# One unit of seven products per feed-forward block in place of two, placed in the middle of the block

## Chip, cores and metric

The kernel runs on one core of a Trainium2 chip. The metric is the device time of one launch in microseconds (us). The stated time of the kernel before is the median of three runs; everything that is read from a trace comes from one profiled execution.

## The reference

Two networks follow one another on 256 tokens of width 1024, all in float32. The first has four layers (a feed-forward block, an attention mixer, a feed-forward block), the second two layers (a mixer, a feed-forward block). The ten feed-forward blocks (FFNs) all compute

```python
def swiglu(x, w_in, w_out):
    gate, up = jnp.split(x @ w_in, 2, axis=-1)      # x: 256 x 1024, w_in: 1024 x 5632
    return (jax.nn.silu(gate) * up) @ w_out          # w_out: 2816 x 1024
```

with a norm before and a norm or a gate after. Eight are those of the first network (`ffn_1`), two those of the second (`ffn_2`). Only they are touched by the change.

## The kernel before, in words

**Numbers in two parts.** A float32 matrix is split into a rounded part `hi` (a cast on ScalarE, L171) and the rest `lo` (a subtraction on VectorE, L172): `hilo`. A product is three matmuls, hi by hi, hi by lo and lo by hi (`mm3`, L215 to L224). Weights come by DMA into a ring of 4 raw buffers of 1 MB (`raw`, issued by SyncE, L182) and are split into a ring of 7 pairs of `hi`/`lo` tiles of 128 x 1024 (`W_BUFS = 7`), from which TensorE reads.

**Chunks.** The hidden width 2816 is cut into 11 chunks of 256. For a chunk `c` and a token tile `t` (two tiles of 128 tokens), `f1(c, t)` makes gate and up with 24 matmuls of 512 columns, `hidden` applies the activation (`th` on ScalarE, two `hd` steps on VectorE) and transposes the result to `hT`, and `f2(c, t)`, called by `pop`, adds the chunk's part of the output with 12 matmuls. A chunk's input weights are 4 tile pairs, its output weights 2.

**Units of seven.** Two neighbouring chunks, 512 columns of gate and 512 of up, can be made together: the two token tiles, the two halves of the depth 1024 and gate/up form a product of 2 x 2 by 2 x 2 blocks, and the generator `seven(c)` makes it with seven block products of 12 matmuls each in place of eight. The left factors, seven sums and differences of the blocks of x in two parts (`S`), are made once per FFN by `halves_of_x` on VectorE and ScalarE. The right factors are made by the DMA itself: a 1 MB quarter of the weights is loaded (`load`, SyncE) and another is added onto it in place (`plus`, two accumulating DMAs of 512 KB issued by GpSimd, L452), for two running buffers `rs` called `y` and `z`; two factors are bare quarters, loaded into the raw ring. A unit thus moves 8 MB where two plain chunks move 4 MB, and splits 14 tile pairs where they split 8. Each `next` of the generator makes one product (its split, its 12 matmuls, and what VectorE and ScalarE add up, gate and multiply behind it).

**Order.** The FFN's order is written out by hand. Chunks 0 and 1 come first, then twice (`PLAN`) a string of steps: two plain chunks and one unit, chunks (2, 3) with the unit 4, 5 and chunks (6, 7) with the unit 8, 9. In the string, `f` is one `f1`, `o` one `pop`, `7` one product of the unit, `n` the first loads of the next unit. Steps n = 7 and n = 15 also take an `ada_step` (1 MB of another weight and four VectorE multiply-adds, L1183; 32 such steps in all, four per FFN from the second FFN to the ninth). `middle()`, called after the first string, loads the gain of the norm after; in the first FFN it also does the late set-up (small DMAs and transposes), in the two of the second network it starts `start_gate`, four more multiply-adds of 1 MB each, spaced by the planner. Chunk 10 and the last output steps end the FFN. Tasks such as `hidden` are resumed by a planner's clock, counted from the matmuls written out so far: `yield 4.0` means 4 us of that clock later. On the engines the instructions do not follow the text strictly: in the trace, matmuls of a product and of a chunk alternate.

Of the kernel before, what the change touches and what calls it, by code (L numbers as in the profile page):

```python
# [18 lines left out]
P = 128  # L19
D = 1024  # L20
S = 256
NT = S // P
# [19 lines left out]
GATE_STEP = 9.0  # L42


PLAN = (((2, 3), 4), ((6, 7), 8))


def _constants():
# [54 lines left out]
class _Net:  # L103
# [296 lines left out]
    def ffn(self, w_in, w_out, factors, finish, middle, scaled):  # L400


        nc = self.nc
        hT, wi, wo, acc = {}, {}, {}, {}

        def f1(c, t):
            self.prepared(t)
            if c not in wi:
                wi[c] = self.load_in(w_in, [(c * FC, FC), (DFF + c * FC, FC)])
            self.start(hidden(c, t, self.project(t, wi[c], 2 * FC)))  # L410

        def hidden(c, t, ps):
            th = self.t(self.fp, [P, FC], "th")
            nc.scalar.activation(th, ps[:, :FC], AF.Tanh, scale=factors(t)[0])
            hd = self.t(self.fp, [P, FC], "hd", bufs=3)
            nc.vector.scalar_tensor_tensor(hd, th, 1.0, ps[:, :FC], op0=ALU.add, op1=ALU.mult)
            nc.vector.scalar_tensor_tensor(hd, hd, factors(t)[1], ps[:, FC:], op0=ALU.mult, op1=ALU.mult)
            yield 4.0
            hT[c, t] = self.to_hT(hd)

        def f2(*cs, t):
            for c in cs:
                if c not in wo:
                    wo[c] = self.load_out(w_out, c)
                self.force(lambda: (c, t) in hT)
            if t not in acc:
                acc[t] = self.accs(t)
            steps = [(hT[c, t], wo[c]) for c in cs]
            if cs[-1] == NCH - 1:
                self.last_steps(acc[t], steps)  # L430
            else:
                self.out_step(acc[t], *steps[0], cs[0] == 0, False)

        def seven(c):

            def quarter(k, n):
                return self.cols(w_in, c * FC + n * DFF, 512, 4 * k, 4)  # L440

            def load(k, n, alone=False):
                if alone:
                    r = self.t(self.wp, [P, 2 * UW], "raw", bufs=RAW_BUFS).rearrange("p (a b) -> p a b", a=4)
                else:
                    r = self.t(self.mp, [P, 4, 512], "rs", bufs=2)
                nc.sync.dma_start(r, quarter(k, n))
                return r

            def plus(r, k, n):  # L450
                for q in range(2):
                    nc.gpsimd.dma_start(r[:, 2 * q : 2 * q + 2], quarter(k, n)[:, 2 * q : 2 * q + 2], accum_op=ALU.add)  # L452

            def split(r):
                ws = []
                for q in range(2):
                    hi = self.t(self.wp, [P, UW], "hi", F32R).rearrange("p (a b) -> p a b", a=2)
                    lo = self.t(self.wp, [P, UW], "lo", F32R).rearrange("p (a b) -> p a b", a=2)
                    self.hilo(r[:, 2 * q : 2 * q + 2], hi, lo)
                    ws += [(hi[:, j], lo[:, j]) for j in range(2)]  # L460
                return ws

            def block(i, ws):
                ps, S = self.ps("mm"), sums["S"]
                x = ([S[0][:, i, k] for k in range(4)], [S[1][:, i, k] for k in range(4)])
                for k in range(4):
                    self.mm3([(ps, slice(0, 512))], x, k, ws[k], k == 0, k == 3)
                return ps

            def add(dst, u, v):  # L470
                nc.vector.tensor_tensor(dst, u, v, op=ALU.add)

            def tile(ps=None):
                r = self.t(self.mp, [P, 512], "sc", bufs=3)
                if ps is not None:
                    nc.scalar.copy(r, ps)
                return r

            def gate(g):
                th = self.t(self.fp, [P, 512], "res", bufs=2)  # L480
                nc.scalar.activation(th, g, AF.Tanh, scale=0.5)
                nc.vector.scalar_tensor_tensor(g, th, 1.0, g, op0=ALU.add, op1=ALU.mult)

            def out(t, g, u):
                nc.vector.scalar_tensor_tensor(u, g, -1.0, u, op0=ALU.mult, op1=ALU.mult)
                yield 6.0
                for i in range(2):
                    hT[c + i, t] = self.to_hT(u[:, FC * i : FC * i + FC])

            y = load(0, 1)  # L490
            plus(y, 0, 0)
            z = load(1, 1)
            yield
            u0 = tile(block(6, split(z)))
            plus(z, 0, 1)
            yield
            u1 = tile(block(3, split(y)))
            plus(y, 1, 1)
            add(u0, u0, u1)
            yield  # L500
            s = tile(block(0, split(load(0, 0, True))))
            yield
            g0 = self.t(self.fp, [P, 512], "res", bufs=2)
            add(g0, block(1, split(load(1, 0, True))), s)
            gate(g0)
            yield
            add(s, block(4, split(y)), s)
            plus(y, 1, 0)
            add(u0, u0, s)
            self.start(out(0, g0, u0))  # L510
            yield
            add(s, block(5, split(z)), s)
            add(u1, s, u1)
            yield
            add(s, block(2, split(y)), s)
            gate(s)
            self.start(out(1, s, u1))
            yield

        queue, sums = [], {}  # L520

        def pop():
            c, t = queue.pop(0)
            f2(c, t=t)

        first = ((0, 0), (0, 1), (1, 0), (1, 1)) if self.stage == 0 else ((0, 0), (1, 0), (0, 1), (1, 1))
        gens = [seven(c) for _, c in PLAN]
        next(gens[0])
        for c, t in first:
            f1(c, t)  # L530
        queue.extend((c, t) for c in range(2) for t in range(NT))
        self.start(self.halves_of_x(sums, scaled))
        for plain, c in PLAN:


            gen, after = gens.pop(0), gens[:1]
            others = [(r, t) for r in plain for t in range(NT)]
            for n, what in enumerate("fo77fo7o7fo7o7foo7no"):
                if what == "f":
                    f1(*others[0])  # L540
                    queue.append(others.pop(0))
                elif what == "o":
                    pop()
                elif what == "n":
                    for g in after:
                        next(g)
                else:
                    self.force(lambda: "S" in sums)
                    next(gen, 0)
                if n in (7, 15) and self.stage > 0:  # L550
                    self.ada_step()
            queue.extend((c + i, t) for i in range(2) for t in range(NT))
            if middle:
                middle()
                middle = None
        for t in range(NT):
            f1(NCH - 1, t)
        for t in range(NT):
            f2(NCH - 3, t=t)
            f2(NCH - 2, NCH - 1, t=t)  # L560
            finish(t, acc[t])
        self.drain()

    def halves_of_x(self, res, scaled):


        nc = self.nc
# [10 lines left out]
        def put(i, v):  # L578
            self.hilo(v, S_[0][:, i], S_[1][:, i])

        f = self.t(self.wp, [P, 2 * UW], "raw", bufs=RAW_BUFS).rearrange("p (a b) -> p a b", a=4)
        x = {}
        for t in (0, 1):
            for k in (0, 1):
# [3 lines left out]
                if not scaled:  # L588
                    nc.vector.tensor_tensor(v, v, rb[:, t, None, :].to_broadcast([P, 4, P]), op=ALU.mult)
        tt, stt = nc.vector.tensor_tensor, nc.vector.scalar_tensor_tensor  # L590
        put(0, x[0, 0])
        put(1, x[0, 1])
        put(2, x[1, 1])
        tt(x[1, 1], x[1, 1], x[1, 0], op=ALU.subtract)
        put(3, x[1, 1])
        tt(x[1, 0], x[0, 0], x[1, 0], op=ALU.subtract)
        put(5, x[1, 0])
        stt(x[0, 0], x[1, 1], -1.0, x[0, 0], op0=ALU.mult, op1=ALU.subtract)
        put(4, x[0, 0])
        stt(x[0, 1], x[0, 0], -1.0, x[0, 1], op0=ALU.mult, op1=ALU.subtract)  # L600
        put(6, x[0, 1])
        res["S"] = S_
        return
        yield
# [1005 lines left out]
```

## Time and profile before

| | |
|---|---|
| median of 3 runs | 2960.28 us (2956.38 to 2962.5) |
| the profiled execution | 2965.05 us, span of its trace 2963.3 us |
| busy: TensorE, VectorE, ScalarE, GpSimd | 2842.5, 2183.1, 1686.3, 427.2 us |
| the ten FFNs together | 1953 us of the span |
| read from HBM | 629.82 MB |

Busy time is the time in which an engine executes something. A window's row gives, for a stretch of the span, the busy time of each engine with its number of instructions, the granted clock of TensorE (1.00 is 2.4 GHz; a stretch that ran partly at 1.2 GHz shows a mean between 0.5 and 1), the busy share of the DMA engines (it can read a little over 1) and the rate. TensorE's busy time includes matmuls that ran at the lower clock, so what a stretch lost on TensorE is its idle time plus the length of the stretch times (1 - granted clock).

### The profile page before, as it was taken

How to read it: one execution, taken by the hardware profiler on the slowest of the kernel's cores; microseconds unless marked ns; L12 is line 12 of the kernel's file. 1: busy time of each engine (PE TensorE's matmuls, PEld its weight loads, DVE VectorE, ACT ScalarE, POOL GpSimd, SP SyncE). 2: the span in 40 equal slices, each digit the busy share in tenths (PEclk: the TensorE clock that was granted, in tenths of full speed). 3: DMA queues.
4: the chain of work that ended last, by engine and by line, in shares of the span. 5: the costliest groups of instructions: out<-in, count | busy, mean ns of one | idle time of the engine just before them, and what ended most of it. 6: DMA issues, size and time to landing. Idle time of an engine off the chain costs nothing. (4 is left out here: it accounts for less than half of the span.)

```text
span 2963.3 us, 36815 instructions
## 1 busy us (share of the span) xinstructions
PE 2842.5 (96%) x13165; PEld 2280.9 (77%) x13165; DVE 2183.1 (74%) x3275; ACT 1686.3 (57%) x2873; POOL 427.2 (14%) x601
## 2 busy tenths in 40 slices
PE   7999999999999999999999999999999998999998
PEld 5787777778787777878778777777778777788777
DVE  7676787877568887756877877587775687765777
ACT  6556655655665565556655556665554464544554
POOL 1112210211111011120211111221101110100110
PEclk9999999999999999999999999999999999999999
DMA  9864588796458879651697895469674599664794
GB/s 262 239 198 155 169 258 237 207 296 206 149 164 256 242 209 291 210 188 44 186 290 227 243 275 173 133 183 291 215 242 169 171 274 267 209 222 164 202 288 142
DMA packets 358043, 633.27 MB, mean 214 GB/s; under 512 B 15170, under 2 KB 190132, under 8 KB 357860
## 3 DMA queue, kind: packets, MB, share of 16 engines
q1 hardware_dynamic: 312724, 541.99, 53.5%
q0 software_dynamic: 44768, 88.30, 16.7%
q8 instruction: 104, 1.70, 0.2%
q14 instruction: 79, 0.65, 0.1%
q10 hardware_dynamic: 368, 0.62, 0.1%
HBM read 629.82 MB, written 1.05 MB: 213 GB/s over the span
## 5 line engine op out<-in xcount | busy, mean ns | idle before, releaser
L172 DVE TENSOR_TENSOR lo<-raw,hi 128x1024 fp32r<-128x1024 f32 x834 | 1000.1, 1220 | 232.5 <-ACT hi L171 223.6
L171 ACT CAST hi<-raw 128x1024 fp32r<-128x1024 f32 x834 | 859.3, 1051 | 322.4 <-PE mm L224 149.0
L220 PE MATMUL mm<-hi,xh 128*128 128x512 f32 (+2 forms) x1856 | 746.1, 404 | 10.3 <-ACT hi L171 5.6
L222 PE MATMUL mm<-lo,xh 128*128 128x512 f32 (+2 forms) x1856 | 730.7, 394 | 3.4 <-DVE lo L172 3.4
L224 PE MATMUL mm<-hi,xl 128*128 128x512 f32 (+2 forms) x1856 | 729.2, 393 | 1.9 <-DVE xl L172 1.0
L220 PEld LDWEIGHTS mm<-hi,xh 128*128 128x128 f32 x1856 | 350.8, 189 | 88.2 <-ACT hi L171 10.1
L224 PEld LDWEIGHTS mm<-hi,xl 128*128 128x128 f32 x1856 | 350.6, 189 | 78.3 <-DVE xl L355 4.8
L222 PEld LDWEIGHTS mm<-lo,xh 128*128 128x128 f32 x1856 | 351.4, 189 | 76.4 <-DVE lo L172 12.3
L171 ACT CAST hi<-rs 128x1024 fp32r<-128x1024 f32 x200 | 209.6, 1048 | 200.4 <-PE mm L224 150.0
L172 DVE TENSOR_TENSOR lo<-rs,hi 128x1024 fp32r<-128x1024 f32 x200 | 243.1, 1220 | 97.4 <-ACT hi L171 97.2
L452 POOL DMA_DIRECT2D rs<-in_ffn_w_in_dram x128 | 155.8, 1274 | 1101.7 <-DVE lo L172 650.9
L220 PE MATMUL mm<-hi,Sh 128*128 128x512 f32 x560 | 231.5, 413 | 13.3 <-ACT Sh L171 10.7
L222 PE MATMUL mm<-lo,Sh 128*128 128x512 f32 x560 | 227.4, 406 | 8.7 <-DVE lo L172 8.7
L224 PE MATMUL mm<-hi,Sl 128*128 128x512 f32 x560 | 224.0, 400 | 0.0
L264 ACT CAST hT<-tp 128x256 fp32r<-128x256 f32 x268 | 94.6, 371 | 204.1 <-PE tp L252 204.0
L222 PE MATMUL aA<-lo,hT 128*128 128x512 f32 x584 | 195.7, 398 | 7.7 <-DVE lo L172 7.7
L220 PE MATMUL aA<-hi,hT 128*128 128x512 f32 x584 | 197.3, 400 | 0.9 <-DVE s L657 0.9
L224 PE MATMUL aA<-hi,hT 128*128 128x512 f32 x584 | 196.2, 400 | 0.0
L222 PE MATMUL aB<-lo,hT 128*128 128x512 f32 x568 | 191.1, 396 | 0.0
L224 PE MATMUL aB<-hi,hT 128*128 128x512 f32 x568 | 190.1, 393 | 0.8 <-DVE hT L268 0.8
L220 PE MATMUL aB<-hi,hT 128*128 128x512 f32 x568 | 190.5, 398 | 0.0
L265 DVE TENSOR_TENSOR hT<-tp,hT 128x256 fp32r<-128x256 f32 x268 | 109.9, 418 | 85.8 <-ACT hT L264 84.5
(280 smaller groups left out, 3671.5 us busy)
## 6 DMA issues: line engine op xcount, KB each, us to landing
raw<-in_ffn_w_in_dram SPq DMA_DIRECT2D x224, 512.0 KB, 6.4
raw<-in_ffn_w_out_dram SPq DMA_DIRECT2D x88, 1024.0 KB, 6.7
rs<-in_ffn_w_in_dram POOLq DMA_DIRECT2D x128, 512.0 KB, 8.2
raw<-in_w_ada_dram SPq DMA_DIRECT2D x48, 1024.0 KB, 7.1
raw<-in_w_in_dram SPq DMA_DIRECT2D x44, 1024.0 KB, 5.2
rs<-in_ffn_w_in_dram SPq DMA_DIRECT2D x32, 1024.0 KB, 6.4
raw<-in_ffn_w_in_dram SPq DMA_DIRECT2D x32, 1024.0 KB, 5.9
raw<-in_w_ffn_in_dram SPq DMA_DIRECT2D x56, 512.0 KB, 5.6
```

Source lines behind the costliest of these rows:

```text
L171: self.nc.scalar.copy(hi, raw)
L172: self.nc.vector.tensor_tensor(lo, raw, hi.bitcast(F32), op=ALU.subtract)
L220: mm(ps, xh[k], wh[:, c], start=first, stop=False)
L222: mm(ps, xh[k], wl[:, c], start=False, stop=False)
L224: mm(ps, xl[k], wh[:, c], start=False, stop=last)
L264: nc.scalar.copy(hi, v)
L265: nc.vector.tensor_tensor(lo, v, hi.bitcast(F32), op=ALU.subtract)
L452: nc.gpsimd.dma_start(r[:, 2 * q : 2 * q + 2], quarter(k, n)[:, 2 * q : 2 * q + 2], accum_op=ALU.add)
```

## The change

`PLAN` becomes `PAIR = 6`: one unit per FFN, chunks 6 and 7; chunks 2, 3, 4, 5, 8 and 9 are plain. Chunks 0 and 1 come first as before; the unit's first loads are issued behind them and no longer ahead of them; chunk 2 follows, then `halves_of_x` is started, then chunk 3, `middle()` and one `ada_step`. Then comes one string of steps with the unit and the plain chunks 4 and 5, which opens with three products of the unit in a row and has one `ada_step`. Chunks 8 and 9 follow, each with an `ada_step` ahead of it. Inside the unit the order of the seven products is new (the two bare quarters first), and the left factors are made in an order that follows it. The wait of `hidden` ahead of its transposes is 6 us of the planner's clock and no longer 4.

```diff
-PLAN = (((2, 3), 4), ((6, 7), 8))
+PAIR = 6
...
             nc.vector.scalar_tensor_tensor(hd, hd, factors(t)[1], ps[:, FC:], op0=ALU.mult, op1=ALU.mult)
-            yield 4.0
+            yield 6.0
             hT[c, t] = self.to_hT(hd)
...
             z = load(1, 1)
             yield
-            u0 = tile(block(6, split(z)))
-            plus(z, 0, 1)
+            g0 = self.t(self.fp, [P, 512], "res", bufs=2)
+            nc.scalar.copy(g0, block(1, split(load(1, 0, True))))
+            yield
+            s = tile(block(0, split(load(0, 0, True))))
+            add(g0, g0, s)
+            gate(g0)
             yield
             u1 = tile(block(3, split(y)))
             plus(y, 1, 1)
-            add(u0, u0, u1)
             yield
-            s = tile(block(0, split(load(0, 0, True))))
-            yield
-            g0 = self.t(self.fp, [P, 512], "res", bufs=2)
-            add(g0, block(1, split(load(1, 0, True))), s)
-            gate(g0)
+            u0 = tile()
+            add(u0, block(6, split(z)), u1)
+            plus(z, 0, 1)
             yield
             add(s, block(4, split(y)), s)
             plus(y, 1, 0)
...
-        gens = [seven(c) for _, c in PLAN]
-        next(gens[0])
+        def plain(*cs):
+            for c in cs:
+                for t in range(NT):
+                    f1(c, t)
+                    queue.append((c, t))
+                    pop()
+
         for c, t in first:
             f1(c, t)
         queue.extend((c, t) for c in range(2) for t in range(NT))
+        gen = seven(PAIR)
+        next(gen)
+        plain(2)
         self.start(self.halves_of_x(sums, scaled))
-        for plain, c in PLAN:
...
-            for n, what in enumerate("fo77fo7o7fo7o7foo7no"):
...
+        plain(3)
+        middle()
+        if self.stage > 0:
+            self.ada_step()
+        others = [(c, t) for c in (PAIR - 2, PAIR - 1) for t in range(NT)]
+
+
+        for n, what in enumerate("fo777fo7fo7fo7ooo7o"):
...
+            if n == 9 and self.stage > 0:
+                self.ada_step()
+        queue.extend((PAIR + i, t) for i in range(2) for t in range(NT))
+        for c in (PAIR + 2, PAIR + 3):
+            if self.stage > 0:
+                self.ada_step()
+            plain(c)
...
+        put(1, x[0, 1])
         put(0, x[0, 0])
-        put(1, x[0, 1])
         put(2, x[1, 1])
         tt(x[1, 1], x[1, 1], x[1, 0], op=ALU.subtract)
         put(3, x[1, 1])
         tt(x[1, 0], x[0, 0], x[1, 0], op=ALU.subtract)
-        put(5, x[1, 0])
         stt(x[0, 0], x[1, 1], -1.0, x[0, 0], op0=ALU.mult, op1=ALU.subtract)
-        put(4, x[0, 0])
         stt(x[0, 1], x[0, 0], -1.0, x[0, 1], op0=ALU.mult, op1=ALU.subtract)
         put(6, x[0, 1])
+        put(4, x[0, 0])
+        put(5, x[1, 0])
```

## Rows read from the trace of the kernel before

**Rows 1.** The page, busy time of each engine over the whole span.

```profile
PE 2842.5 (96%) x13165; PEld 2280.9 (77%) x13165; DVE 2183.1 (74%) x3275; ACT 1686.3 (57%) x2873; POOL 427.2 (14%) x601
```

**Rows 2.** Windows over the ten FFNs: the fifth, and all together.

```profile
1060.00:1255.00 195.00, 187.54 (x833) 149.95 (x832) 157.03 (x216) 111.72 (x164) 26.70 (x35) 0.99 0.78 233
...
sum 1953.00, PE 1879.95 PEld 1502.71 DVE 1561.25 ACT 1101.40 POOL 264.84; mean PE 188.00 PEld 150.27 DVE 156.13 ACT 110.14 POOL 26.48
```

**Rows 3.** Windows 26 to 45 us after the start of each FFN.

```profile
369.00:388.00 19.00, 15.83 (x57) 12.05 (x57) 14.42 (x24) 8.38 (x14) 2.51 (x2) 0.82 0.46 154
566.00:585.00 19.00, 15.83 (x62) 11.81 (x61) 15.22 (x25) 9.29 (x16) 3.06 (x3) 0.91 0.46 148
...
sum 189.00, PE 168.57 PEld 127.15 DVE 158.11 ACT 99.64 POOL 34.93; mean PE 16.86 PEld 12.72 DVE 15.81 ACT 9.96 POOL 3.49
```

**Rows 4.** Windows in the fifth FFN: its first 40 us, and 58 to 80 us.

```profile
1060.00:1084.00 24.00, 23.87 (x113) 18.82 (x112) 22.18 (x39) 15.76 (x33) 3.16 (x7) 1.00 0.59 190
1084.00:1100.00 16.00, 12.83 (x52) 9.76 (x52) 15.11 (x26) 8.61 (x15) 0.81 (x1) 0.91 0.37 124
...
1118.00:1140.00 22.00, 20.02 (x86) 15.58 (x85) 17.52 (x22) 12.26 (x15) 2.39 (x2) 1.00 1.06 330
```

**Rows 5.** Timeline of the second FFN: start, duration, instruction, [idle before, releaser].

```profile
378.99 0.50 PE L220 MATMUL mm<-hi,Sh 128*128 128x512 f32 x1 [1.78 <-ACT Sh L171]
...
381.33 1.22 PE L222 MATMUL aA<-lo,hT 128*128 128x512 f32 x2 [1.30 <-DVE lo L172]
```

**Rows 6.** Groups by line: count, busy, mean ns, idle before.

```profile
L172 DVE TENSOR_TENSOR lo<-rs,hi 128x1024 fp32r<-128x1024 f32 x200 | 243.1, 1220 | 97.4 <-ACT hi L171 97.2
...
L1183 DVE SCALAR_TENSOR_TENSOR ada<-raw,col,ada 128x512 f32<-128x512 f32 x112 | 78.3, 745 | 26.5 <-DMA raw<-in_w_ada_dram 26.5
...
L417 DVE SCALAR_TENSOR_TENSOR hd<-hd,fs,mm 128x256 f32<-128x256 f32 x112 | 53.3, 476 | 1.9
...
L172 DVE TENSOR_TENSOR Sl<-raw,Sh 128x512 fp32r<-128x512 f32 x70 | 46.3, 684 | 4.7 <-ACT Sh L171 4.7
```

**Rows 7.** Timeline of TensorE: a run of 18 plain matmuls, then one of 12.

```profile
393.00 0.39 PE L220 MATMUL mm<-hi,xh 128*128 128x512 f32 x1
...
396.86 0.40 PE L224 MATMUL mm<-hi,xl 128*128 128x512 f32 x1
...
402.86 0.40 PE L220 MATMUL mm<-hi,Sh 128*128 128x512 f32 x1
...
405.42 0.40 PE L224 MATMUL mm<-hi,Sl 128*128 128x512 f32 x1
```

**Rows 8.** The page's DMA queues: packets, MB, share of the 16 engines' span.

```profile
q1 hardware_dynamic: 312724, 541.99, 53.5%
q0 software_dynamic: 44768, 88.30, 16.7%
```

**Rows 9.** Windows 58 to 80 us after each FFN's start, summed, then 80 to 92.

```profile
sum 220.00, PE 209.38 PEld 164.71 DVE 179.76 ACT 122.11 POOL 25.31; mean PE 20.94 PEld 16.47 DVE 17.98 ACT 12.21 POOL 2.53
...
sum 120.00, PE 120.00 PEld 97.53 DVE 112.98 ACT 81.45 POOL 23.06; mean PE 12.00 PEld 9.75 DVE 11.30 ACT 8.15 POOL 2.31
```

**Rows 10.** Windows 92 to 125 us: first FFN, ninth, all ten.

```profile
117.00:150.00 33.00, 29.71 (x119) 21.93 (x118) 17.53 (x27) 15.36 (x21) 4.82 (x4) 0.90 0.74 190
...
2444.00:2477.00 33.00, 27.62 (x117) 22.04 (x116) 24.32 (x31) 15.33 (x20) 4.85 (x4) 0.95 0.94 254
...
sum 329.00, PE 306.57 PEld 242.38 DVE 227.22 ACT 172.75 POOL 48.29; mean PE 30.66 PEld 24.24 DVE 22.72 ACT 17.27 POOL 4.83
```

**Rows 11.** Windows 125 to 150 us after each FFN's start: ninth FFN, all ten.

```profile
2477.00:2502.00 25.00, 21.31 (x83) 16.98 (x82) 18.11 (x25) 9.50 (x13) 1.38 (x2) 0.86 0.97 313
...
sum 251.00, PE 246.40 PEld 199.08 DVE 207.01 ACT 127.42 POOL 23.09; mean PE 24.64 PEld 19.91 DVE 20.70 ACT 12.74 POOL 2.31
```

**Rows 12.** Timeline of the fifth FFN, 105 to 110 us after its start.

```profile
1165.33 1.41 DVE L1183 SCALAR_TENSOR_TENSOR ada<-raw,col,ada 128x512 f32<-128x512 f32 x2 [4.39 <-DMA raw<-in_w_ada_dram]
...
1169.72 0.41 PE L252 MATMUL tp<-cst,hd 128*128 128x128 f32 x2 [2.18 <-DVE hd L417]
```

More of the change, by code (lines that the diff above doesn't have):

```diff
@@ L531, in ffn @@
         queue.extend((c, t) for c in range(2) for t in range(NT))
+        gen = seven(PAIR)
+        next(gen)
+        plain(2)
         self.start(self.halves_of_x(sums, scaled))
-        for plain, c in PLAN:
-            gen, after = gens.pop(0), gens[:1]
-            others = [(r, t) for r in plain for t in range(NT)]
-            for n, what in enumerate("fo77fo7o7fo7o7foo7no"):
[L539 to L555, printed above, removed]
+        plain(3)
[4 more added lines that the diff above has]
+        for n, what in enumerate("fo777fo7fo7fo7ooo7o"):
+            if what == "f":
+                f1(*others[0])
+                queue.append(others.pop(0))
+            elif what == "o":
+                pop()
+            else:
+                self.force(lambda: "S" in sums)
+                next(gen, 0)
+            if n == 9 and self.stage > 0:
[5 more added lines that the diff above has]
+            plain(c)
         for t in range(NT):
```

## The prediction

> **What bounds the kernel now.** I read the page's busy times first, then windows over the ten FFNs, then windows by stretch, then the timeline where a stretch loses time. TensorE is busy 96% of the span, VectorE 74% [rows 1], so nearly every instruction taken from or given to TensorE counts. But 96% is an average. The ten FFNs take 1953 us and TensorE is busy in 1880 of them: 73 us idle [rows 2]. To that comes time in which the granted clock was 1.2 GHz, which the windows count as busy.
>
> The loss has places, and I give each as idle time plus length times (1 - clock):
> - 26 to 45 us after an FFN's start: idle 189.0 - 168.6 = 20.4 us; the clock is 0.82 in two of the ten windows and 0.91 in four, so 19 x (2 x 0.18 + 4 x 0.09) = 13.7 us. Together 34.1 us [rows 3].
> - 58 to 80 us: 10.6 us idle [rows 9].
> - 92 to 125 us: 22.4 us idle, and 33 x (0.10 + 2 x 0.05) = 6.6 us by the clock (0.90 in the first FFN, 0.95 in two others): 29.0 us [rows 10]. 125 to 150 us: 4.6 us idle, and 25 x 0.14 = 3.5 us in the ninth FFN: 8.1 us [rows 11]. Together 37.1 us, of which the first FFN has 3.3 + 3.3 = 6.6 and the ninth 5.4 + 1.65 + 3.7 + 3.5 = 14.2.
>
> These three sum to 81.8 us. Of the 73 us of idle time they hold 20.4 + 10.6 + 22.4 + 4.6 = 58; 15 us lie elsewhere, and I leave them as they are.
>
> The first loss is VectorE's. In the first 40 us of the fifth FFN it is busy 22.18 of 24 and 15.11 of 16 us, and the DMA engines only 0.59 and 0.37 [rows 4]: it splits weights for chunks 0 to 2 and builds the left factors. TensorE then waits for a left factor (1.78 us) and for the next `lo` (1.30 us) [rows 5], and behind these gaps its clock falls to 1.2 GHz [rows 3]. The second loss lies where the DMA share is 1.06 at 330 GB/s [rows 4]: transfers are the limit there. The third is seen at 1165 us: VectorE stands 4.39 us before an `ada` step whose 1 MB has not landed; the `hd` step is queued behind it, and TensorE waits 2.18 us for its transposes [rows 12].
>
> **The change, part by part.**
>
> *TensorE gets more.* Per FFN 7 products of 12 matmuls go and 8 of 12 come. A plain matmul takes (396.86 - 393.00)/17 = 0.227 us, one of a unit (405.42 - 402.86)/11 = 0.2327 us [rows 7]. So 96 x 0.227 - 84 x 0.2327 = 21.8 - 19.5 = +2.25 us, over ten FFNs **+22.5 us**. This is certain, and nothing hides it, as it is TensorE's own.
>
> *VectorE and ScalarE get less.* The unit's 14 `lo` steps become 8: 6 x 1.22 = 7.3 us [rows 6]. Its 11 steps of 512 columns (seven sums, four of gate and result) cost about 11 x 0.684 = 7.5 us, taking the 512-column row; the plain chunks' eight `hd` steps cost at most 8 x 0.476 = 3.8 us [rows 6]. VectorE thus loses some 11 us of work per FFN, of 156 [rows 2]; ScalarE falls in step. Neither is worth time by itself; it is worth what TensorE waited for it.
>
> *The DMA gets less.* The accumulating queue took 16.7% of 2963 us for 88.3 MB, 5.6 us per MB; the other 53.5% for 542 MB, 2.9 us per MB [rows 8]. In its string of steps the kernel before moves 14 loads and 4 accumulations of 1 MB: 14 x 2.9 + 4 x 5.6 = 63 us, against 276 matmuls x 0.23 = 63.5 us. That is no slack, as the share of 1.06 says. In the new string 11 loads and 3 accumulations stand: 32 + 17 = 49 us against the same 63.5.
>
> *The left factors come later.* They are 19 steps of 512 columns on VectorE in eight FFNs, 19 x 0.684 = 13 us, and 15 in the other two [rows 6]. Before, they had the cover of chunks 0 and 1; now chunk 2 with two `pop` stands ahead: 72 matmuls, 16.3 us of TensorE, with 6 x 1.22 + 4 x 0.476 = 9.2 us of VectorE (and two `lo` of `hT`, which I leave inside the margin). VectorE gains some 6 to 7 us, against the 3.2 us that TensorE idled [rows 4]. So the gap should close with some 3 us to spare, and with it the fall of the clock. What is late next is chunk 3 and the opening of the unit: chunk 3 (9.2 us), one `ada` step (3.0), chunk 4 (4.9 + 1.0), a `pop` (2.4) and three products in a row (6 x 1.22 + two steps of 0.684 = 8.7) ask 29 us of VectorE while TensorE has 72 + 72 matmuls, 32.8 us. That is tight but not over. I keep 7 of 34.1 us: **-27 us**. Bounds: 0 to -34.
>
> *58 to 80 us.* Half of it should go with the DMA's relief: **-5.5 us**, bounds 0 and -10.6.
>
> *92 to 150 us.* There is no second unit. The late set-up of the first FFN stays, only earlier (6.6 us). In the ninth and tenth the four gate steps now start ahead of the only unit; I keep 9 of the ninth's 14.2. Four `ada` steps per FFN remain, one inside the unit; each is in VectorE's order, with `hd` steps and splits behind it, for which TensorE waits. With a DMA that has slack I keep some 3.5 us in all others. 37.1 - 19 = **-18 us**, bounds 0 and -37.
>
> *Edits at nothing.* `yield 6.0`: the transposes come later in the text, and the queue of four finished pieces ahead of `pop` covers it; bounds from nothing to 2.18 us where they now are asked for too early [rows 12], so if anything it gains. The unit's first loads move behind chunks 0 and 1 on SyncE's queue, and the accumulations with them on GpSimd's: the DMA share there is 0.4 to 0.6 [rows 4], so chunk 2's weights are not pushed out. Between two uses of `y` or `z` there are now never fewer than 84 matmuls, 19 us; the closest pair before had 72, in a stretch without any idle time [rows 9]. The orders of the products and of the left factors change no count.
>
> *Sum.* 22.5 - 27 - 5.5 - 18 = -28 us. The profiled execution took 2965.05 us for a span of 2963.3 us; the median is 4.8 us below it. I apply the difference to the median: 2960.3 - 28, about **2932 us**.
>
> **The rivals.**
>
> *The wait moves (slower).* The 13 us of the left factors fall on VectorE just ahead of the unit's opening, where I count 29 us of work for 32.8 us of TensorE. If VectorE enters that stretch without a lead, TensorE stands before the second and third product in each FFN, and the clock falls as it does now. At the present price, 34.1 us over ten FFNs, the 27 us are not gained and 22.5 - 5.5 - 18 = -1 us is left; with 4.3 us per FFN it is +8 us, 2968. It decides at about 2.8 us per FFN (28 us over ten), and means slower by more than 0.2% at 3.4. For it: VectorE's 93% [rows 4]. Against: 72 matmuls more of lead, and a DMA that can fill the raw ring.
>
> *TensorE is the bound, its waits are not the unit's (slower).* If every gap belongs to the left factors, the `ada` steps and the set-up, which all stay, only the 22.5 us remain: 2983 us. For it: 96% [rows 1]. Against: the gaps' places, which follow the two units. A page speaks for this rival: the Trainium skill, Perfetto Trace Analysis, section Identifying the Most-Contended Engine, says to relieve first the engine of highest occupancy, and to judge TensorE by its weight loads. By that rule, with weight loads at 77% against VectorE's 74% [rows 1], a change that hands TensorE work makes the kernel slower; the same page allows that the contended engine changes over time, and the stretches here do [rows 4].
>
> *Only the left factors' gap closes.* If the losses from 58 us on are those of `ada`, gate and set-up, they come back elsewhere: 22.5 - 27 - 3 = -8 us, 2952. For it: the wait at 1165 us is an `ada` step's [rows 12]. Against: that step was late in a stretch where the DMA was full.
>
> *Nearly all goes.* 22.5 - 81.8 = -59 us, 2901. For it: the calm 80 to 92 us [rows 9]. Against: the set-up and the gate remain.
>
> **Chances.** The forecast 0.52, only the first gap 0.20, the wait moves 0.15, TensorE 0.05, nearly all 0.08. What a measurement of this kernel tells from no change is about 0.2%, 6 us. The forecast, nearly all and two thirds of the third lie below 2954: faster 0.73. The rest of that one and part of the moved wait give same 0.10; slower 0.17. The range reaches from near "nearly all" to the upper part of the moved wait, 2904 to 2966; outside lie the second rival, the tail of the first and half of the last. The forecast's own range is 2914 to 2946.
>
> **What the profile after would show.** TensorE with 12 more matmuls of 512 columns per FFN, 120 in all; `lo<-rs` halved to 100; in windows before the unit no wait of TensorE for a left factor, and the clock at 1.00 there; DMA share below 1 in the unit. Wrong would be: TensorE waiting for `lo` at the unit's opening with the clock down; `ada` waits as long as now; a new wait for `y` or `z`.

## The result: 2929 us, about as forecast, but not by the steps of the forecast

The changed kernel takes 2929.28 us (median of four runs, 2926.22 to 2933.07) against 2961.39 us; the ratio is 0.9887, with a 95% interval of 0.9869 to 0.9905. The forecast was 2932 us. The profiled execution has a span of 2924.4 us, 38.9 us less than before.

The page of the kernel after, busy times and the two large DMA queues:

```profile
PE 2839.6 (97%) x13285; PEld 2297.3 (79%) x13285; DVE 2081.9 (71%) x3185; ACT 1622.7 (55%) x2803; POOL 334.0 (11%) x521
...
q1 hardware_dynamic: 333844, 542.00, 54.8%
q0 software_dynamic: 23008, 46.36, 8.4%
```

TensorE has 120 instructions more, as counted, and VectorE 101 us less work. Windows of the kernel after, counted from the starts of its own FFNs as in [rows 3, 9 to 11]: 26 to 45 us, 58 to 80 us, 92 to 125 us (first FFN, third FFN, sum), 125 to 150 us, and the ten FFNs:

```profile
sum 190.00, PE 190.00 PEld 156.34 DVE 143.17 ACT 93.19 POOL 0.00; mean PE 19.00 PEld 15.63 DVE 14.32 ACT 9.32 POOL 0.00
...
sum 220.00, PE 214.97 PEld 166.05 DVE 167.15 ACT 128.34 POOL 28.03; mean PE 21.50 PEld 16.61 DVE 16.71 ACT 12.83 POOL 2.80
...
106.00:139.00 33.00, 33.00 (x149) 26.48 (x147) 22.36 (x29) 16.11 (x21) 2.40 (x2) 1.00 0.77 219
...
616.00:649.00 33.00, 28.92 (x120) 23.05 (x119) 24.59 (x32) 14.59 (x18) 2.41 (x2) 0.90 0.71 221
...
sum 330.00, PE 303.02 PEld 242.30 DVE 260.50 ACT 155.43 POOL 24.01; mean PE 30.30 PEld 24.23 DVE 26.05 ACT 15.54 POOL 2.40
...
sum 250.00, PE 250.00 PEld 205.92 DVE 170.36 ACT 121.83 POOL 21.65; mean PE 25.00 PEld 20.59 DVE 17.04 ACT 12.18 POOL 2.17
...
sum 1925.00, PE 1884.97 PEld 1524.69 DVE 1466.02 ACT 1045.54 POOL 173.56; mean PE 188.50 PEld 152.47 DVE 146.60 ACT 104.55 POOL 17.36
```

Two stretches that the prediction left as they are, the first 26 us and 45 to 58 us of the ten FFNs, before (first and third line) and after:

```profile
sum 260.00, PE 249.45 PEld 198.93 DVE 233.09 ACT 167.07 POOL 39.68; mean PE 24.94 PEld 19.89 DVE 23.31 ACT 16.71 POOL 3.97
...
sum 260.00, PE 253.99 PEld 202.91 DVE 228.59 ACT 172.21 POOL 43.75; mean PE 25.40 PEld 20.29 DVE 22.86 ACT 17.22 POOL 4.38
...
sum 131.00, PE 128.61 PEld 103.82 DVE 104.84 ACT 72.37 POOL 12.95; mean PE 12.86 PEld 10.38 DVE 10.48 ACT 7.24 POOL 1.29
...
sum 130.00, PE 130.00 PEld 106.79 DVE 114.18 ACT 78.98 POOL 0.00; mean PE 13.00 PEld 10.68 DVE 11.42 ACT 7.90 POOL 0.00
```

Read with the same rule, idle time plus length times (1 - clock):

| stretch | before | after | forecast of the difference | measured |
|---|---|---|---|---|
| 26 to 45 us | 34.1 | 0 | -27 | -34 |
| 58 to 80 us | 10.6 | 5.0 | -5.5 | -5.6 |
| 92 to 150 us | 37.1 | 27.0 + 11.6 = 38.6 | -18 | +1.5 |
| first 26 us | 14.2 | 7.8 | none | -6.4 |
| 45 to 58 us | 2.4 | 0 | none | -2.4 |
| first matmul of the first FFN | 18.6 | 12.1 | none | -6.6 |

(The 11.6 us: the clock is 0.95 in three of the ten windows from 92 to 125 us and 0.90 in two, 33 x 0.35. In the first 26 us it is 0.93 in two FFNs before, 3.6 us, and in one after, 1.8 us.) The ten FFNs give back 1953 - 1925 = 28 us between the marks from which their windows are counted, and 11 us lie ahead of the first mark, 25 us before and 14 us after. But these two marks are not at the same matmul: 16 matmuls of the first FFN lie ahead of the one and 3 ahead of the other, and its first matmul comes 6.6 us earlier. The first row went further than forecast, the third did not come at all, and the last three had no line in the sum.

What TensorE waits for in the third stretch, from the timeline of the fifth FFN of the kernel after, some 90 to 102 us after its start:

```profile
1132.63 0.37 SPq L1184 DMA_DIRECT2D raw<-in_w_ada_dram  x1
...
1141.35 2.74 DVE L1192 SCALAR_TENSOR_TENSOR ada<-raw,col,ada 128x512 f32<-128x512 f32 x4 [3.98 <-DMA raw<-in_w_ada_dram]
...
1142.21 0.40 PE L224 MATMUL mm<-hi,xl 128*128 128x512 f32 x1
...
1145.28 0.50 PE L222 MATMUL mm<-lo,Sh 128*128 128x512 f32 x1 [2.67 <-DVE lo L172]
```

It is the picture of [rows 12] with another last link. The ada step's 1 MB is issued at 1132.63 and usable at 1141.35; VectorE stands 3.98 us before it, multiplies for 2.74 us, and only then makes the `lo` for the next product, for which TensorE waits 2.67 us. What the same `lo` waits for otherwise is ScalarE's `hi`, here in the fifth FFN and, where no ada step stands between, in the first:

```profile
1140.10 1.05 ACT L171 CAST hi<-rs 128x1024 fp32r<-128x1024 f32 x1 [3.69 <-PE mm L224]
...
1144.01 2.35 DVE L172 TENSOR_TENSOR lo<-rs,hi 128x1024 fp32r<-128x1024 f32 x2
...
115.14 2.59 DVE L172 TENSOR_TENSOR lo<-rs,hi 128x1024 fp32r<-128x1024 f32 x2 [3.08 <-ACT hi L171]
```

So VectorE would have stood until 1141.15 in any case, and with the load in time the 2.74 us of multiplying would have fitted into that wait; as the load landed only then, they stand between `hi` and `lo`. Each FFN from the second to the eighth has one such stop of TensorE, of 2.7 to 4.9 us, always for this `lo`; the longest is in the eighth, where the load landed 2.4 us after `hi` was ready. The first and the tenth FFN, which have no ada step, lose nothing in this stretch; the third has a stop of 4.1 us and a fall of the clock to 0.90.

The start, SyncE's timeline of the kernel after, and the first matmul of the first FFN before and after:

```profile
1.63 11.03 SPq L182 DMA_DIRECT2D raw<-in_ffn_w_in_dram  x8
12.77 2.80 SPq L447 DMA_DIRECT2D rs<-in_ffn_w_in_dram  x2
...
18.61 1.22 PE L220 MATMUL mm<-hi,xh 128*128 128x512 f32 x2 [5.01 <-ACT hi L171]
...
12.05 0.79 PE L220 MATMUL mm<-hi,xh 128*128 128x512 f32 x1 [4.36 <-ACT hi L171]
```

Eight weight loads of chunks 0 and 1 now go out ahead of the unit's two megabytes.

### The profile page after: what moved, and what is told of

The parts are those of the page before. It is cut to its first block, busy times and chain, and to the rows that moved or that the text cites. A ratio compares the mean times of both kernels' runs of the same rounds, so it can differ in the third digit from the quotient of the medians.

```text
span 2924.4 us, 36751 instructions
## 1 busy us (share of the span) xinstructions
PE 2839.6 (97%) x13285; PEld 2297.3 (79%) x13285; DVE 2081.9 (71%) x3185; ACT 1622.7 (55%) x2803; POOL 334.0 (11%) x521
## 3 DMA queue, kind: packets, MB, share of 16 engines
q1 hardware_dynamic: 333844, 542.00, 54.8%
q0 software_dynamic: 23008, 46.36, 8.4%
## 4 chain that ended last, share of the span: by engine, by line
PE 82%; DVE 7%; ACT 3%; DMA 3%; issue 2%; POOL 2%; SPq 0%; DVEq 0%; POOLq 0%; ACTq 0%
PE mm L222 17%; PE mm L224 17%; PE mm L220 16%; PE tp L252 4%; PE aA L222 4%; PE aA L220 4%; PE aA L224 4%; DVE lo L172 4%; PE aB L220 3%; PE aB L222 3%; PE aB L224 3%; DMA raw<-in_w_ada_dram 3%; ACT hi L171 1%; PE aA L1088 1%; DVE res L382 1%
## 5 line engine op out<-in xcount | busy, mean ns | idle before, releaser
L220 PE MATMUL mm<-hi,xh 128*128 128x512 f32 x2176 | 878.2, 405 | 7.4 <-ACT hi L171 4.4
L224 PE MATMUL mm<-hi,xl 128*128 128x512 f32 x2176 | 855.5, 393 | 1.8 <-DVE xl L172 0.8
L222 PE MATMUL mm<-lo,xh 128*128 128x512 f32 x2176 | 855.8, 393 | 0.5 <-DVE lo L172 0.5
L222 PEld LDWEIGHTS mm<-lo,xh 128*128 128x128 f32 x2176 | 413.3, 190 | 81.0 <-DVE lo L172 5.2
L452 POOL DMA_DIRECT2D rs<-in_ffn_w_in_dram x64 | 78.7, 1294 | 870.6 <-DVE lo L172 622.7
L171 ACT CAST hi<-rs 128x1024 fp32r<-128x1024 f32 x100 | 102.9, 1049 | 95.1 <-PE mm L224 91.2
L222 PE MATMUL mm<-lo,Sh 128*128 128x512 f32 x280 | 115.3, 412 | 30.5 <-DVE lo L172 30.4
L414 ACT ACTIVATE th<-mm,fs 128x256 f32<-128x256 f32 x144 | 68.3, 474 | 128.1 <-PE mm L224 128.0
L224 PEld LDWEIGHTS aA<-hi,hT 128*128 128x128 f32 x584 | 109.6, 188 | 24.0
L222 PEld LDWEIGHTS aA<-lo,hT 128*128 128x128 f32 x584 | 109.5, 188 | 23.8 <-DVE lo L172 0.8
```

Source lines behind the costliest of these rows:

```text
L171: self.nc.scalar.copy(hi, raw)
L220: mm(ps, xh[k], wh[:, c], start=first, stop=False)
L222: mm(ps, xh[k], wl[:, c], start=False, stop=False)
L224: mm(ps, xl[k], wh[:, c], start=False, stop=last)
```

## The experiments

Theory, as it stood after the result: the gap of the left factors closed because they are started later; the loss at 92 to 125 us is VectorE standing before the ada load; the start is the order of SyncE's queue. The rivals stand in the expectations. The kernel before was timed again beside each run, 2963.6 to 2964.0 us, and each ratio is to that time.

### The unit's first loads ahead of chunk 0 again (e1)

```diff
+        gen = seven(PAIR)
+        next(gen)
         for c, t in first:
             f1(c, t)
...
-        gen = seven(PAIR)
-        next(gen)
```

> Kernel after, with the unit's first loads back ahead of chunk 0. Theory (the first loads stood ahead of the first weights on SyncE's queue): the start of the first FFN goes back from 14.3 us to about 25 us, so +10 us, near 2940 us, and at most 3 us more at the starts of the other FFNs. Rival (all the gain is in the middle of the FFNs, the order of the first loads is hidden): within 3 us of the kernel after, 2929.

Measured: 2935.02 us, ratio to the kernel before 0.9903 (0.9886 to 0.9919), 6 us above the kernel after. SyncE's timeline of this run:

```profile
1.63 0.43 SPq L182 DMA_DIRECT2D raw<-in_ffn_w_in_dram  x1
5.97 0.92 SPq L447 DMA_DIRECT2D rs<-in_ffn_w_in_dram  x2
6.94 23.37 SPq L182 DMA_DIRECT2D raw<-in_ffn_w_in_dram  x11
```

Its first matmul of the first FFN:

```profile
18.89 1.22 PE L220 MATMUL mm<-hi,xh 128*128 128x512 f32 x2 [5.19 <-ACT hi L171]
```

After one weight load the two `rs` loads stand in front again, and the first matmul comes 6.8 us later than in the kernel after. The 10 us of the theory were read between two marks that are not at the same matmul. So the order is worth some 6 to 7 us; the two intervals overlap, and the place of the gain rests on the timeline.

### The kernel before with only that part of the change (e4)

```diff
-        next(gens[0])
         for c, t in first:
             f1(c, t)
         queue.extend((c, t) for c in range(2) for t in range(NT))
+        next(gens[0])
```

> Kernel before, with nothing changed but the unit's first loads behind chunks 0 and 1. Theory: the first FFN starts some 10 us earlier, and the rest stays: 2948 to 2953 us. Rival (the later loads make the first product of the first unit wait, which takes back the gain): within 4 us of the kernel before, 2961.

Measured: 2959.12 us against 2963.99, ratio 0.9986 (0.9976 to 0.9996). The first FFN's first matmul comes at 12.70 us, 5.9 earlier than in the kernel before, and some 5 us are left in the time, half of what the theory said. The time by itself also lies in the range of the rival; in the first FFN, 26 to 45 us after its mark, 4.4 us are lost against 0.7 before, and whether the late loads cause that was not shown.

### The left factors started ahead of chunk 2 (e2)

```diff
+        self.start(self.halves_of_x(sums, scaled))
         plain(2)
-        self.start(self.halves_of_x(sums, scaled))
```

> Kernel after, with the left factors started ahead of chunk 2 as before. Theory (VectorE lacks a lead there): the gap of 34 us over ten FFNs with its fall of the clock comes back, at least 20 us of it: 2950 to 2963 us. Rival (the gap closed because the FFN has less to split and to transfer, not because the factors moved): within 5 us of 2929.

Measured: 2926.0 us, ratio 0.9879 (0.9865 to 0.9894): no difference from the kernel after. Windows 26 to 45 us of this run, summed:

```profile
sum 190.00, PE 189.41 PEld 154.99 DVE 182.35 ACT 113.83 POOL 0.00; mean PE 18.94 PEld 15.50 DVE 18.24 ACT 11.38 POOL 0.00
```

VectorE is at 182 of 190 us, so the factors are built there, and TensorE loses 0.6 us. The theory falls: where the factors start does not decide by itself. The rival, that one unit asks less than two, is tried in the next run.

### The one unit in the place of the first unit of before (e8)

```diff
-PAIR = 6
+PAIR = 4
...
-        plain(2)
         self.start(self.halves_of_x(sums, scaled))
-        plain(3)
-        middle()
-        if self.stage > 0:
-            self.ada_step()
...
-        for c in (PAIR + 2, PAIR + 3):
-            if self.stage > 0:
+        middle()
+        for c in range(PAIR + 2, PAIR + 6):
+            if self.stage > 0 and c < PAIR + 5:
                 self.ada_step()
             plain(c)
```

> Kernel after with its one unit where the first unit of the kernel before was: chunks 4 and 5 made together right behind chunks 0 and 1, chunks 2 and 3 in its string, chunks 6 to 9 plain behind it. Theory (the gap closed because the first product now comes 33 us later): the gap at 26 to 45 us and its fall of the clock come back, 15 to 34 us, 2943 to 2963 us. Rival (it closed because one unit asks less than two): within 6 us of 2929.

Measured: 2986.14 us, ratio 1.0076 (1.0053 to 1.0099), slower than the kernel before. Windows of this run: 26 to 45 us (third FFN, sum), 58 to 80 us (sum):

```profile
565.00:584.00 19.00, 15.38 (x57) 11.59 (x55) 14.09 (x22) 8.16 (x15) 0.00 (x0) 0.82 0.50 170
...
sum 190.00, PE 160.84 PEld 121.89 DVE 154.23 ACT 96.65 POOL 0.91; mean PE 16.08 PEld 12.19 DVE 15.42 ACT 9.67 POOL 0.09
...
sum 220.00, PE 184.85 PEld 145.58 DVE 145.10 ACT 76.67 POOL 24.02; mean PE 18.48 PEld 14.56 DVE 14.51 ACT 7.67 POOL 2.40
```

The gap is back, 29 us idle with the clock at 0.82 to 0.91 in six of the ten FFNs, and the loss of the unit's later products has moved forward with the unit to 58 to 80 us, which takes the time above the theory's range. With e2 this settles the first row of the table: it is the place of the first product in the FFN. In the fifth FFN the last left factor is made 36 us after the start in the kernel before, in e2 and in this run, and 53 us after it in the kernel after; the first product comes at 35, 67, 31 and 66 us. Where it comes at 31 to 35 us VectorE has no lead; at 66 us it has, wherever the factors stand in the text.

### The wait of hidden at 4 us (e6)

```diff
-            yield 6.0
+            yield 4.0
             hT[c, t] = self.to_hT(hd)
```

> Kernel after with the wait of hidden at 4 us as before. Theory (an edit at nothing): within 5 us of 2929. Rival (the later transposes are what closed the gap of the left factors): 2945 us or more, with waits of TensorE for hd at 26 to 45 us.

Measured: 2933.58 us, ratio 0.9896 (0.9878 to 0.9914). Within the uncertainty of the kernel after, with 1.1 us idle at 26 to 45 us over ten FFNs; nothing of the gap hangs on it.

### Ada steps that do not wait for their load (e7)

```diff
         nc.sync.dma_start(rv, src)
+        if other is not None:
+            rv = other[:, None, :].to_broadcast([P, 2, D])
...
-        self.ada_add(self.ada_acc, l, i, u, u == 0)
+        self.ada_add(self.ada_acc, l, i, u, u == 0, self.h[1])
```

> Kernel after whose ada steps load their 1 MB as before but multiply and add from the resident h, so that VectorE no longer stands before the load; same instructions, same transfers, other numbers in that sum. Theory (VectorE standing before the ada load is the wait at 97 to 105 us): the loss at 92 to 125 us falls from 38 to under 12 us, 2898 to 2912 us. Rival (the split waits for the accumulation into its running buffer, or for the ring): the loss stays above 25 us, time above 2920 us.

Measured: 2892.23 us, ratio 0.9759 (0.9743 to 0.9774), 37 us below the kernel after. Windows 92 to 125 us, summed:

```profile
sum 330.00, PE 327.24 PEld 263.12 DVE 244.18 ACT 180.82 POOL 15.62; mean PE 32.72 PEld 26.31 DVE 24.42 ACT 18.08 POOL 1.56
```

27.0 us idle become 2.8, and the clock falls in one window only; the time is below the theory's range. The accumulations are the same, so the running buffers `y` and `z` are not what is waited for. But the order on VectorE is not the same: in the fifth FFN all ada multiply-adds now run 11 to 65 us after its start, none in the unit, and from 92 to 125 us VectorE has 16 us less to do over ten FFNs. So this run takes away the wait and the multiplying together, and does not tell one from the other.

### One ada step moved out of the unit (e3)

```diff
-            if n == 9 and self.stage > 0:
-                self.ada_step()
...
             plain(c)
+        if self.stage > 0:
+            self.ada_step()
```

> Kernel after, with the ada step of n = 9 moved out of the unit, behind chunk 9. Theory (at 97 to 105 us the step's 1 MB lands late, VectorE stands before it, and the split for the next product behind it): the 38 us lost at 92 to 125 us after the starts fall under 10 us, time 2895 to 2910 us. Rival (the product waits for the accumulation into its own running buffer): the wait of TensorE for lo stays at 3 to 5 us in each of these FFNs, time within 6 us of 2929.

Measured: 2929.71 us, ratio 0.9881 (0.9865 to 0.9898): nothing. Timeline of the fifth FFN (start at 1043 us) of this run:

```profile
1139.85 2.74 DVE L1192 SCALAR_TENSOR_TENSOR ada<-raw,col,ada 128x512 f32<-128x512 f32 x4 [6.12 <-DMA raw<-in_w_ada_dram]
...
1142.96 0.48 DVE L417 SCALAR_TENSOR_TENSOR hd<-hd,fs,mm 128x256 f32<-128x256 f32 x1
1143.36 1.22 DVE L172 TENSOR_TENSOR lo<-rs,hi 128x1024 fp32r<-128x1024 f32 x1
...
1143.59 0.47 PE L220 MATMUL mm<-hi,xh 128*128 128x512 f32 x1 [3.48 <-DVE hd L417]
```

An ada step stands in the unit all the same, 6.12 us idle before it, with an `hd` step and a `lo<-rs` behind it; TensorE now waits 3.48 us for the `hd`. In the text this step is the one ahead of chunk 8, behind the whole unit: the order on VectorE is not that of the text. The four ada steps of this FFN start on VectorE at 53, 86, 98 and 118 us in the kernel after, and at 53, 97, 119 and 136 us here. So the step moved away, that of n = 9, was the one at 86 us, where TensorE has no stop; the step that stops it, at 98 us in the kernel after, was that ahead of chunk 8 already there, and was not moved.

### All later ada steps behind chunk 8 (e9)

```diff
-            if n == 9 and self.stage > 0:
-                self.ada_step()
...
         for c in (PAIR + 2, PAIR + 3):
+            plain(c)
             if self.stage > 0:
                 self.ada_step()
-            plain(c)
+        if self.stage > 0:
+            self.ada_step()
```

> Kernel after with one ada step behind chunk 3 as it is, one behind chunk 8 and two behind chunk 9, none in or right behind the unit; it computes the reference. Theory (the ada wait at 97 to 105 us was worth 37 us, and behind chunk 8 the transfers have room): 2892 to 2905 us. Rival (the order on VectorE is not that of the text, and the step comes forward into the unit again, as with one step less moved): 2920 to 2932 us.

Measured: 2889.46 us (2888.76 to 2891.89), ratio 0.9755 (0.9738 to 0.9771). Its ada sums are those of the kernel after, which e7's are not; it takes 40 us less, 2.5 us below the theory's range. Windows 92 to 125 us, and the ten FFNs:

```profile
sum 330.00, PE 330.00 PEld 265.45 DVE 266.86 ACT 182.75 POOL 15.81; mean PE 33.00 PEld 26.54 DVE 26.69 ACT 18.27 POOL 1.58
...
sum 1892.00, PE 1878.32 PEld 1519.25 DVE 1464.87 ACT 1048.49 POOL 173.39; mean PE 187.83 PEld 151.93 DVE 146.49 ACT 104.85 POOL 17.34
```

No idle time is left in the stretch that lost 38.6 us. In the fifth FFN the four ada steps now start on VectorE at 53, 116, 133 and 141 us, none from 80 to 115 us. VectorE has no less to do in this stretch than in the kernel after (266.86 against 260.50 us): what counts is the place of the steps in its order.

### The kernel before with ada steps that do not wait (e10)

The edit of e7, on the kernel before.

> Kernel before whose ada steps load as before but compute from the resident h, as in the like run of the kernel after. Theory (the loss at 92 to 125 us of the kernel before was the ada steps' too, not the second unit's): 15 to 25 us faster than before, 2936 to 2948 us, and the gap of the left factors stays. Rival (the second unit's transfers set that loss): within 6 us of 2962.

Measured: 2957.6 us against 2963.99, ratio 0.9982 (0.9969 to 0.9995): 6 us less, neither the 15 to 25 us nor nothing, though the time by itself lies in the range of the rival. Windows 26 to 45 us and 92 to 125 us, summed:

```profile
sum 190.00, PE 158.09 PEld 119.64 DVE 171.69 ACT 93.20 POOL 26.04; mean PE 15.81 PEld 11.96 DVE 17.17 ACT 9.32 POOL 2.60
...
sum 330.00, PE 318.32 PEld 251.02 DVE 221.43 ACT 178.26 POOL 48.61; mean PE 31.83 PEld 25.10 DVE 22.14 ACT 17.83 POOL 4.86
```

The late stretch does fall, from 22.4 us idle to 11.7. But the order on VectorE changed as well: it has 14 us more to do from 26 to 45 us [rows 3], and the gap of the left factors grows from 20.4 to 31.9 us idle. In the fifth FFN all ada multiply-adds now run 16 to 71 us after its start. By the rule of the table the loss from 92 to 150 us falls from 37.1 to 15.8 us. So some half of the late loss went with the ada steps; as the order changed with the edit, what they cost in the kernel before is not shown more closely.

### No unit at all (e5)

```diff
-        gen = seven(PAIR)
-        next(gen)
-        plain(2)
-        self.start(self.halves_of_x(sums, scaled))
-        plain(3)
+        plain(2, 3)
         middle()
+        for c in range(4, NCH - 1):
+            if self.stage > 0 and c % 2 == 0:
+                self.ada_step()
+            plain(c)
         if self.stage > 0:
             self.ada_step()
...
```

(The rest of the cut takes out the string of steps and chunks 8 and 9 behind it.)

> Kernel after without any unit of seven: chunks 2 to 9 all plain, no left factors, the four ada steps spread over chunks 4, 6, 8 and the end. Theory (the trade goes on as it did: 22.5 us of matmuls more, against what the unit still loses): the 5 us at 58 to 80 us and most of the 38 us at 92 to 125 us go, near 2915 us. Rival (those losses belong to the ada steps and stay with them): 2940 to 2952 us.

Measured: 2892.87 us, ratio 0.976 (0.9745 to 0.9776). It beats the change by 36 us, with 120 matmuls more by the count of the products. Windows 58 to 80 and 92 to 125 us:

```profile
sum 220.00, PE 220.00 PEld 179.54 DVE 148.67 ACT 89.98 POOL 1.86; mean PE 22.00 PEld 17.95 DVE 14.87 ACT 9.00 POOL 0.19
...
sum 330.00, PE 330.00 PEld 271.25 DVE 210.74 ACT 151.22 POOL 0.00; mean PE 33.00 PEld 27.13 DVE 21.07 ACT 15.12 POOL 0.00
```

TensorE never stands in either. Against the kernel with all later ada steps behind chunk 8 (2889.46 us) the unit of seven is worth 3.4 us of the 22.5 us of matmuls that it saves; the ranges of the two kernels (2888.76 to 2891.89 and 2890.4 to 2893.94) overlap by 1.5 us, so even the sign is close. Over the ten FFNs the one loses 15.5 us by the rule of the table and the other 9.0, which is 6.5 us of the missing 19; where the rest goes is not shown. The ada steps stand at other places in the two kernels, so not all of the difference need be the unit's.

## Why the prediction came out

**Right in time and direction, with errors that cancelled.** The sum was 22.5 - 27 - 5.5 - 18 = -28 us, measured -32 by the medians and -38.9 between the two profiled executions. The 18 us that did not come were made up by places that had no line or a smaller one: 7 us more at 26 to 45 us, 9 us in the two stretches left as they are, 7 us at the start; some 6 of TensorE's 22.5 us did not come either. That the time came out is luck; that the change is faster by closing the first gap is not.

**TensorE's +22.5 us.** The count, 12 matmuls more per FFN, is in the page. Its price can't be read off alone. An estimate from the windows: without all their losses the ten FFNs hold 1852.5 us before and 1871.6 after, 19 us more, less 3 us for the 13 matmuls by which the first marks differ; so some 16 us.

**The left factors, -27: right in size, wrong in cause.** The gap closed wholly, 34 us. I put it down to where the factors are started; e2 starts them early and loses 0.6 us, e8 puts the first product early and loses 47.6 us there (29.2 idle, 18.4 by the clock). What counts is how much VectorE has gained by the time that the product is due. The lead that I counted (72 matmuls with little to split) was the right quantity, credited to the wrong instruction.

**58 to 80 us, -5.5.** Measured -5.6, but as the fall of half the loss with the DMA's relief it is not shown. The stretch now holds the opening of the unit where it held the middle of one, and the waits there are for VectorE and ScalarE: in the fifth FFN 1.1 us for `lo` and 0.9 for `sc` before, 0.5 for `lo` after.

**92 to 150 us, -18: wrong.** "With a DMA that has slack I keep some 3.5 us in all others" failed. The mean had slack, 49 us of transfers in 63.5; the moment had not: the ada load was in flight for 8.7 us beside accumulations and weight loads, and VectorE, which stood 3.98 us before it, came 4.7 us after its issue. The window ahead of it, 80 to 92 us of the fifth FFN, and VectorE's waits for ada loads over the span (us in all, times, longest):

```profile
1123.00:1135.00 12.00, 12.00 (x55) 9.78 (x54) 12.00 (x17) 7.52 (x9) 1.69 (x2) 1.00 1.10 248
...
DVE ada L1192 <- DMA raw<-in_w_ada_dram: 37.1, 10, 6.2
```

A DMA share of 1.10 in the unit, and ada waits of 37.1 us where they were 26.5 [rows 6]: of the prediction's own signs the first did not come and the second, a sign of being wrong, did. The count of "one inside the unit" failed too: two of the four steps run there on VectorE. The rival "only the left factors' gap closes" had this part right: its mechanism was the ada step, and e9 shows it.

**A bound of a rival.** That the moved wait "means slower by more than 0.2% at 3.4" us per FFN is a slip: by the same sum, 3.4 us gives no change, and 4.1 us the 6 us of 0.2%.

**Edits at nothing.** Right for `yield` (e6) and for the spacing of `y` and `z` (e9 keeps it and loses nothing from 92 to 150 us). Wrong for the unit's first loads: I priced them by the DMA share at the start of the fifth FFN, where there is room, and not at the kernel's start, where the first splits wait for the first weights. Worth 5 to 7 us net (e1, e4).

**The rule against the change.** The Trainium skill, Perfetto Trace Analysis, section Identifying the Most-Contended Engine, says to optimize the engine of highest occupancy first. Taken, as I took it for the rival, to mean that a change which loads that engine costs time, it fails here twice: 32 us faster with 120 more matmuls, and 2892.87 us with both units gone, 240 more than before by the count of the products. The advice of the Trainium skill on the same page, section Optimization Strategy, to find the gaps on that engine and what releases them is what e7 and e9 followed, and there the trace agrees: 40 us.

**Left open.** Why the order on the engines moves the ada steps forward was not tried; what takes back most of the 22.5 us of the unit where no late wait is left (e9 against e5) was not found; how the late loss of the kernel before divides between ada steps and second unit is only bounded (e10).

## What to carry to other kernels

A unit that saves matmuls need not be worth its count; here seven products for eight gave 3.4 us of 22.5, even with the late waits gone. A small task on a shared engine, waiting for a load of its own, held up what stood behind it here: look at what heads the engine's queue when TensorE stops, not at the engine's busy share, and ask whether the task would have cost anything had its load been in time. Before moving a task, find in the trace which one stops the engine: e3 moved another. And a transfer's room is to be judged in the few microseconds in which it is due, not by the mean of its stretch.

## What was unexpected of the hardware

An ada load of 1 MB took 8.7 us from issue (1132.63) to the first use (1141.35), where the median of that group is 5.3 us in the same kernel. The queue of the accumulating transfers kept its price with half the volume: 8.4% of 2924 us for 46.36 MB, 5.3 us per MB where it was 5.6, against 54.8% for 542 MB, 3.0 us per MB (4.4 MB in that queue are others: they are left in e5, without any unit). With some short stops of TensorE its clock went down: the third FFN, with one of 4.1 us from 92 to 125 us, was granted 0.90 there, part of the stretch at 1.2 GHz, the fifth, with one of 2.7 us, and the first, with none, 1.00; and with the idle time gone (all later ada steps behind chunk 8) every such window has 1.00.
